# Second mixer of a two-layer block: the context's cumulative gates by a scan of products instead of a doubling ladder

## Chip, core and metric

The kernel runs on one core of one Trainium2 chip. The metric is device time of that core in microseconds (us), the median of the runs of one kernel.

The engines are named as the profile names them: PE (TensorE matmuls; PEld its weight loads), DVE (VectorE), ACT (ScalarE), POOL (GpSimd) and SP (which issues the DMAs). Each takes its instructions in the order in which the program lists them, so an instruction that waits holds back all that stand behind it on its engine.

## What is computed

The reference runs two transformer blocks of two layers each over 256 latent and 256 context tokens, 1024 wide. The change is in the second layer of the first block, whose mixer is a gated linear recurrence, forward and backward, with eight heads of 128 (cut to what matters):

```python
def _odd_mixer(h_ctx, h_lat, w_in, lower_bounds, layer, out_norm, ctx_out):
    fq, f_fwd, f_bwd, fi, fog = _split(h @ w_in, ODD_SIZES)
    q = _heads(jax.nn.silu(fq), HGRN_HEADS)
    ...
    for d, f in enumerate((f_fwd, f_bwd)):
        log_f = ...                       # log of a gate between lb and 1
        k = -jnp.expm1(log_f)
        dirs.append(_directional_scan(q, k, i, log_f, n_ctx, reverse=(d == 1)))
    ...
# recurrence in each direction:  S_t = diag(exp(g_t)) S_{t-1} + k_t v_t^T,  o_t = S_t^T q_t
# the context is scanned first from a zero state, the latent tokens go on from its final state
```

Only the latent outputs are wanted in this layer. Of the context, then, only the final state counts: the sum over its tokens of k times v, each k multiplied by all gates that come after it in the direction of the recurrence. That running product of gates over the 256 context tokens is what is computed in another way.

## The kernel before

The eight heads are worked off as four pairs. In `odd_mixer`, `proj(p)` multiplies the tokens by the weights of pair p. Its projections are fp32, made of two reduced-precision parts each: ACT casts a weight tile `raw` to `hi` (L203), DVE subtracts to get `lo` (L204), and PE runs three matmuls for each (L213 to L215; L285, L287 and L288 with the tokens as the stationary side). Out of each projection of gates ACT makes two sigmoids (L818). DVE turns them into the gates `ac` (context) and `al` (latent) on L824, and into the keys `Kc` and `Kl` on L822. Each of these tiles holds two directions, two heads and 256 tokens: 4 x 256 numbers in each of 128 partitions. `late(p)` projects the output gate and the values; PE's matmuls L337 of a stream of modulation weights (`mraw`, two buffers, 512 KB each) lie between the projections.

`hgrn_pair(p, ...)` is a ladder of eight levels. At level `lev` tokens are taken in blocks of m = 2^lev. For the latent tokens each level makes a tile of scores on PE (L909), copies it under a mask into `S` (DVE, L911), and multiplies `Kl` (L914) and `Q2` (L923) by the products of gates over a block, `tl`. For the context the same ladder runs on POOL: at each level `Kc` is multiplied by the products over blocks, `tc_` (L924), and the products are halved in number by multiplying neighbours (L929, on POOL for `tc_`, on DVE for `tl`). After eight levels each `Kc` has been multiplied by all gates behind it. POOL also adds the two directions of `Kl` (`ks`, L889). Once the ladder is through, PE multiplies `Kc` by `Q2` (L944, L945), and the read-out follows.

A scheduler sets the order of the instructions of each engine when the program is built; Python's order is only its starting point. The ladders of pairs 0 and 1 run while PE projects for the pairs behind them; the ladders of pairs 2 and 3 run interleaved with one another and with `late(2)` and `late(3)`.

Of the kernel before, what the change touches and what calls it, by code (L numbers as in the profile page):

```python
# [9 lines left out]
F32 = mybir.dt.float32  # L10
# [3 lines left out]
ALU = mybir.AluOpType  # L14
# [3 lines left out]
P = 128  # L18
# [19 lines left out]
def vw(ap, off, dims):  # L38
    return bass.AP(ap.tensor, ap.offset + off, [ap.ap[0]] + [list(d) for d in dims])
# [97 lines left out]
class Kern:  # L137
# [741 lines left out]
    def hgrn_pair(self, p, al, ac, Kl, Kc, Q2, q, V, sog, gain, mix):  # L879
        nc = self.nc  # L880
        mm = nc.tensor.matmul
        DS = 512

        def g2(name):
            return mix.tile([P, 2, 256], F32, tag=name, name=self.n(name), bufs=2)

        S = g2("S")
        ks = mix.tile([P, 2, 256], F32, tag="S256", name=self.n("ks"), bufs=2)
        nc.gpsimd.tensor_tensor(ks, Kl[:, 0], Kl[:, 1], ALU.add)  # L889
        ps = self.psum("pa")  # L890
        for h in range(2):
            for tt in range(2):
                ts = slice(tt * P, (tt + 1) * P)
                mm(ps[:, h * 256 + tt * P:h * 256 + (tt + 1) * P], ks[:, h, ts], q[:, h, ts], start=True, stop=True)
        nc.scalar.copy(S.rearrange("p h n -> p (h n)"), ps)
        for d in range(2):
            nc.vector.tensor_tensor(Q2[:, d], q, al[:, d], ALU.mult)
        tl = al.rearrange("p d h n -> p (d h n)")
        tc_ = ac.rearrange("p d h n -> p (d h n)")
        for lev in range(8):  # L900
            m = 1 << lev
            nb = DS // (2 * m)
            pat = [[2 * m, nb], [DS + m, 2], [1, m]]
            if lev < 7:
                KC = g2("KC").rearrange("p h n -> p (h n)")
                nc.scalar.copy(vw(KC, 0, [[2 * m, nb], [m, 2], [1, m]]), vw(Kl, 0, pat))
                ps = self.psum("pa")
                for b in range(4):
                    mm(ps[:, b * P:(b + 1) * P], KC[:, b * P:(b + 1) * P],  # L909
                       vw(Q2, b * P, [[2 * m, 64 // m], [DS + m, 2], [1, m]]), start=True, stop=True)  # L910
                nc.vector.copy_predicated(S.rearrange("p h (t i) -> p (h t) i", t=2),  # L911
                                          self.masks[:, lev, None, :].to_broadcast([P, 4, P]),
                                          ps.rearrange("p (t i) -> p t i", t=4))
                nc.vector.tensor_tensor(vw(Kl, 0, pat), vw(Kl, 0, pat), self.dyadic(m, DS, nb, tl, "k"), ALU.mult)  # L914
            else:
                S128 = g2("S128")
                ps = self.psum("pa")
                for h in range(2):
                    o = h * 256
                    mm(ps[:, o + P:o + 256], Kl[:, 0, h, :P], Q2[:, 1, h, P:], start=True, stop=True)  # L920
                    mm(ps[:, o:o + P], Kl[:, 1, h, P:], Q2[:, 0, h, :P], start=True, stop=True)
                nc.scalar.copy(S128.rearrange("p h n -> p (h n)"), ps)
            nc.vector.tensor_tensor(vw(Q2, 0, pat), vw(Q2, 0, pat), self.dyadic(m, DS, nb, tl, "q"), ALU.mult)  # L923
            nc.gpsimd.tensor_tensor(vw(Kc, 0, pat), vw(Kc, 0, pat), self.dyadic(m, DS, nb, tc_, "k"), ALU.mult)  # L924
            if lev < 7:
                for w, eng in (("l", nc.vector), ("c", nc.gpsimd)):
                    t2 = mix.tile([P, 2, nb], F32, tag=f"tot{w}{lev}", name=self.n("tot"), bufs=2)
                    pr = vw(tl if w == "l" else tc_, 0, [[DS // m, 2], [2, nb], [1, 2]])
                    eng.tensor_tensor(t2, pr[:, :, :, 0], pr[:, :, :, 1], ALU.mult)  # L929
                    t2 = t2.rearrange("p d n -> p (d n)")  # L930
                    if w == "l":
                        tl = t2
                    else:
                        tc_ = t2
            yield
        tag = "pl" if p > 1 else "pb"
        ss = self.psum("pb")
        oS = []
        for h in range(2):
            ps = self.psum(tag)  # L940
            for j in range(2):
                js = slice(j * P, (j + 1) * P)
                o = ps[:, j * 256:(j + 1) * 256]
                mm(o, Kc[:, 0, h, js], Q2[:, 1, h], start=True, stop=False)  # L944
                mm(o, Kc[:, 1, h, js], Q2[:, 0, h], start=False, stop=True)  # L945
            S256 = mix.tile([P, 512], F32, tag="S256", name=self.n("S256"), bufs=2)
            nc.scalar.copy(S256, ps)
            po = self.psum("pa")
            vs = slice((2 * p + h) * P, (2 * p + h + 1) * P)
            for j in range(2):  # L950
                mm(po[:, :256], V[:, j, vs], S256[:, j * 256:(j + 1) * 256], start=j == 0, stop=False,
                   skip_group_check=True)
            for tt in range(2):
                ts = slice(tt * P, (tt + 1) * P)
                mm(po[:, ts], V[:, 2 + tt, vs], S[:, h, ts], start=False, stop=False, skip_group_check=True)
                mm(po[:, ts], V[:, 3 - tt, vs], S128[:, h, ts], start=False, stop=True, skip_group_check=True)
            oS.append(self.gated_readout_rows(po[:, :256], h, gain, mix, ss))
            yield
        r = self.sm.tile([P, 8], F32, tag="rs16", name=self.n("rs"))
        self.rstd_rows(ss[:, :4], P, 4, r[:, :4])  # L960
        yield
        for h in range(2):
            bc = self.psum(tag)
            for tt in range(2):
                mm(bc[:, tt * P:(tt + 1) * P], r[:, tt * 2 + h:tt * 2 + h + 1].to_broadcast([P, P]), self.ident,
                   start=True, stop=True)
            hd = 2 * p + h
            nc.vector.tensor_tensor(oS[h], oS[h], bc[:, :256], ALU.mult)
            nc.gpsimd.tensor_tensor(sog[:, hd], oS[h], sog[:, hd], ALU.mult)
# [1172 lines left out]
```

## Time and profile before

| | |
|---|---|
| median of 3 runs | 2533.04 us (2531.86 to 2533.44) |
| the profiled execution | 2535.2 us |
| its span, from first to last instruction | 2533.4 us |
| PE busy | 2379.4 us, 94% |
| DVE busy | 1522.6 us, 60% |
| ACT busy | 967.0 us, 38% |
| POOL busy | 509.0 us, 20% |

The profiled execution is 2.2 us longer than the median and 1.8 us longer than its own span, so a difference taken from the trace can be set against the median as it stands. The ladders of the four pairs lie between about 890 and 1165 us of the span. In rows of the timeline the first two numbers are start and duration in us, "xN" is a merged run of N instructions, and square brackets give how long the engine had been idle and what ended that.

### The profile page before, as it was taken

Reading aid. Unit: us, or ns where it says so; the run is one execution under the profiler, and the core shown is the slowest. Engines: PE = TensorE matmul, PEld = TensorE weight load, DVE = VectorE, ACT = ScalarE, POOL = GpSimd, SP = SyncE. Lnnn points to the kernel's source line nnn. Section 1 sums busy time; section 2 is a strip of 40 time slices with the busy share of each in tenths; the row PEclk is TensorE's granted clock in tenths of the full one; section 3 lists DMA queues with packets and bytes.
Section 4 is the critical chain, followed back from the end, with each engine's and each line's share of the span. In section 5 each row is a group of like instructions: output and inputs, shape, how many; then the busy total and the mean of one; then the engine's idle time right before and its main releaser. Section 6 shows DMA issues by size and latency. Waiting matters only on the chain.

```text
span 2533.4 us, 40092 instructions
## 1 busy us (share of the span) xinstructions
PE 2379.4 (94%) x15813; PEld 1959.2 (77%) x15813; DVE 1522.6 (60%) x2897; ACT 967.0 (38%) x1591; POOL 509.0 (20%) x648
## 2 busy tenths in 40 slices
PE   7999988999999888889999999999999999858999
PEld 5875566888888668889799797556888889628999
DVE  5545446778853646684555642765688734586666
ACT  5523323322222423334444443443423224535543
POOL 3910012556630232230100100110000000360000
PEclk9999998999999899999999999999999999979999
DMA  8326672556553252213865432002455533976554
GB/s 295 116 90 233 219 278 61 163 164 174 155 144 95 89 190 67 75 45 141 293 187 182 170 108 67 17 18 73 140 181 179 177 100 98 210 256 224 159 184 150
DMA packets 162925, 378.05 MB, mean 149 GB/s; under 512 B 24144, under 2 KB 70096, under 8 KB 162608
## 3 DMA queue, kind: packets, MB, share of 16 engines
q1 hardware_dynamic: 159728, 368.27, 45.8%
q0 software_dynamic: 3008, 7.21, 1.0%
q8 instruction: 125, 2.05, 0.3%
q14 instruction: 64, 0.52, 0.1%
HBM read 344.75 MB, written 30.67 MB: 148 GB/s over the span
## 4 chain that ended last, share of the span: by engine, by line
PE 48%; DVE 9%; DMA 3%; ACT 2%; issue 2%; POOL 0%; DVEq 0%; ACTq 0%; POOLq 0%
PE pl L214 12%; PE pl L213 12%; PE pl L215 11%; DMA mcol<-ada_t 2%; DVE lo L204 2%; PE pm L337 1%; DVE pm L403 1%; PE pa L909 1%; PE pl L992 1%; PE pl L287 1%; PE pa L1023 1%; DMA mraw<-ada_w 1%; PE pl L285 1%; PE pl L288 1%; PE pb L1289 1%
## 5 line engine op out<-in xcount | busy, mean ns | idle before, releaser
L203 ACT CAST hi<-raw 128x1024 fp32r<-128x1024 f32 (+4 forms) x393 | 400.3, 1020 | 840.1 <-PE pl L214 510.0
L204 DVE TENSOR_TENSOR lo<-raw,hi 128x1024 fp32r<-128x1024 f32 (+4 forms) x393 | 495.7, 1263 | 348.5 <-ACT hi L203 346.3
L214 PE MATMUL pl<-X,hi 128*128 128x256 f32 (+1 forms) x2032 | 649.5, 321 | 6.5 <-POOL X L498 5.8
L213 PE MATMUL pl<-X,hi 128*128 128x256 f32 (+1 forms) x2032 | 651.9, 323 | 2.1 <-ACT X L495 1.9
L215 PE MATMUL pl<-X,lo 128*128 128x256 f32 (+1 forms) x2032 | 647.0, 319 | 0.0
L214 PEld LDWEIGHTS pl<-X,hi 128*128 128x128 f32 x2032 | 392.3, 193 | 40.1 <-POOL X L498 8.7
L213 PEld LDWEIGHTS pl<-X,hi 128*128 128x128 f32 x2032 | 391.4, 193 | 39.8 <-issue 9.0
L215 PEld LDWEIGHTS pl<-X,lo 128*128 128x128 f32 x2032 | 392.3, 193 | 32.4 <-issue 6.6
L214 PE MATMUL pl<-hl,hi 128*128 128x256 f32 (+1 forms) x1071 | 327.0, 306 | 6.6 <-DVE hl L1721 6.5
L213 PE MATMUL pl<-hh,hi 128*128 128x256 f32 (+1 forms) x1071 | 327.6, 307 | 4.7 <-ACT hh L1720 4.6
L215 PE MATMUL pl<-hh,lo 128*128 128x256 f32 (+1 forms) x1071 | 325.6, 305 | 0.0
L213 PEld LDWEIGHTS pl<-hh,hi 128*128 128x128 f32 x1071 | 202.4, 189 | 20.8 <-ACT hh L1720 5.8
L214 PEld LDWEIGHTS pl<-hl,hi 128*128 128x128 f32 x1071 | 202.7, 189 | 18.1 <-DVE hl L1721 8.4
L215 PEld LDWEIGHTS pl<-hh,lo 128*128 128x128 f32 x1071 | 202.9, 190 | 10.3 <-issue 0.8
L337 PE MATMUL pm<-mraw,s_cc 128*32 128x512 f32 x576 | 120.0, 618 | 13.2 <-DMA mraw<-ada_w 13.0
L1513 POOL TENSOR_TENSOR Ec<-PGr,bc 128x576 f32<-128x576 f32 x64 | 94.9, 1494 | 170.3 <-DMA bc<-s_w 89.1
L213 PE MATMUL pl<-M,hi 128*128 128x256 f32 (+1 forms) x416 | 122.9, 298 | 6.1 <-ACT hi L203 5.2
L215 PE MATMUL pl<-M,lo 128*128 128x256 f32 (+1 forms) x416 | 122.3, 296 | 1.2 <-DVE lo L204 1.2
L214 PE MATMUL pl<-M,hi 128*128 128x256 f32 (+1 forms) x416 | 122.6, 296 | 0.2 <-DVE M L864 0.2
L498 POOL TENSOR_TENSOR X<-nt,X 128x256 fp32r<-128x256 f32 x48 | 37.9, 790 | 415.3 <-ACT nt L497 415.3
L403 DVE SCALAR_TENSOR_TENSOR pm<-mcol,mrow 128x512 f32<-128x512 f32 x128 | 89.3, 698 | 33.3 <-DMA mcol<-ada_t 22.5
L1734 DVE TENSOR_TENSOR y<-y,pl 128x256 f32<-128x256 f32 (+1 forms) x86 | 45.1, 525 | 102.1 <-PE pl L215 101.6
(515 smaller groups left out, 3710.7 us busy)
## 6 DMA issues: line engine op xcount, KB each, us to landing
mraw<-mod_w SPq DMA_DIRECT2D x96, 512.0 KB, 5.9
raw<-f_u SPq DMA_DIRECT2D x88, 512.0 KB, 4.3
mraw<-ada_w SPq DMA_DIRECT2D x64, 512.0 KB, 6.3
raw<-p_u SPq DMA_DIRECT2D x64, 512.0 KB, 3.7
raw<-p_d SPq DMA_DIRECT2D x64, 512.0 KB, 3.6
raw<-ow_fm SPq DMA_DIRECT2D x32, 512.0 KB, 3.3
mcol<-ada_t SPq DMA_DIRECT2D x64, 256.0 KB, 3.0
raw<-f_d SPq DMA_DIRECT2D x32, 448.0 KB, 3.3
```

Of the source, the lines that this page charges most:

```text
L203: nc.scalar.copy(hi, raw)
L204: nc.vector.tensor_tensor(lo, raw, f32(hi), ALU.subtract)
L213: mm(out, w[0][:, kw, wsl], xh, start=first and a == 0, stop=False, skip_group_check=True)
L214: mm(out, w[0][:, kw, wsl], xl, start=False, stop=False, skip_group_check=True)
L215: mm(out, w[1][:, kw, wsl], xh, start=False, stop=last and a == nk - 1, skip_group_check=True)
L285: mm(o, X[0][:, kk, ts], w[0][:, k, :], start=kk == 0 and tt % per == 0, stop=False, skip_group_check=True)
L287: mm(o, X[0][:, kk, ts], w[1][:, k, :], start=False, stop=False, skip_group_check=True)
L337: nc.tensor.matmul(ps[32 * j:32 * j + 32, :], s[:, k, :], raw[:, jj * 512:(jj + 1) * 512], start=k == 0, stop=k == KT - 1, skip_group_chec ...
L403: nc.vector.scalar_tensor_tensor(self.psum("pm"), buf[:, n % 2], 1.0, s[:, v], ALU.mult, ALU.mult, accum_out=(dst if h else part)[:, v, j: ...
L498: nc.gpsimd.tensor_tensor(lo[:, k, a:b], t, f32(hi[:, k, a:b]), ALU.subtract)
L1513: nc.gpsimd.tensor_tensor(Ec[i], ff[i], cs[i], ALU.mult)
L1734: nc.vector.tensor_tensor(y[:, c, a0:b0], y[:, c, a0:b0], ps, ALU.add)
```

## The change

The context's ladder is taken out of all eight levels: POOL no longer multiplies `Kc` at each level (8 instructions for each pair) and no longer halves `tc_` (7 for each pair). In its place DVE runs four scans for each pair, one for each direction and head. A scan goes over 255 of the 256 context gates, forward for direction 0 and backward for direction 1, and replaces each by the product of itself with all before it; the second operand of the scan is a column of ones. Then POOL multiplies the keys of one direction by these products, both heads at once, shifted by one token: two instructions for each pair. In Python this stands at levels 3 and 5. The latent ladder and all matmuls are as before.

```diff
             nc.vector.tensor_tensor(vw(Q2, 0, pat), vw(Q2, 0, pat), self.dyadic(m, DS, nb, tl, "q"), ALU.mult)
-            nc.gpsimd.tensor_tensor(vw(Kc, 0, pat), vw(Kc, 0, pat), self.dyadic(m, DS, nb, tc_, "k"), ALU.mult)
             if lev < 7:
-                for w, eng in (("l", nc.vector), ("c", nc.gpsimd)):
-                    t2 = mix.tile([P, 2, nb], F32, tag=f"tot{w}{lev}", name=self.n("tot"), bufs=2)
-                    pr = vw(tl if w == "l" else tc_, 0, [[DS // m, 2], [2, nb], [1, 2]])
-                    eng.tensor_tensor(t2, pr[:, :, :, 0], pr[:, :, :, 1], ALU.mult)
...
+                t2 = mix.tile([P, 2, nb], F32, tag=f"totl{lev}", name=self.n("tot"), bufs=2)
+                pr = vw(tl, 0, [[DS // m, 2], [2, nb], [1, 2]])
+                nc.vector.tensor_tensor(t2, pr[:, :, :, 0], pr[:, :, :, 1], ALU.mult)
+                tl = t2.rearrange("p d n -> p (d n)")
+            if lev in (3, 5):
+
+                d = lev // 2 - 1
+                for h in range(2):
+                    a = vw(ac, d * DS + h * 256 + 255 * d, [[1 - 2 * d, 255]])
+                    nc.vector.tensor_tensor_scan(a, a, self.ones[:, :1].to_broadcast([P, 255]), 1.0, ALU.mult, ALU.mult)
+                ks, gs = slice(1 - d, 256 - d), slice(d, 255 + d)
+                nc.gpsimd.tensor_tensor(Kc[:, 1 - d, :, ks], Kc[:, 1 - d, :, ks], ac[:, d, :, gs], ALU.mult)
```

The lines behind it shift by one or less (L909 becomes L908, L911 becomes L910, L923 becomes L922). The order of the instructions moves in three places that matter below. In the listings a row is line, operation, output tile, input tiles and shape; the last number in a tile's name counts the tiles of the program.

POOL, the context ladder of pair 1. Before, its first part:

```order
L929 TENSOR_TENSOR tot_9122<-ac_8126 128x512
L929 TENSOR_TENSOR tot_9137<-tot_9122 128x256
L924 TENSOR_TENSOR Kc_8128<-Kc_8128,ac_8126 128x256x2
L929 TENSOR_TENSOR tot_9152<-tot_9137 128x128
L924 TENSOR_TENSOR Kc_8128<-Kc_8128,tot_9122 128x128x2x2
L929 TENSOR_TENSOR tot_9167<-tot_9152 128x64
L924 TENSOR_TENSOR Kc_8128<-Kc_8128,tot_9137 128x64x2x4
L929 TENSOR_TENSOR tot_9182<-tot_9167 128x32
L924 TENSOR_TENSOR Kc_8128<-Kc_8128,tot_9152 128x32x2x8
```

Of the 15 instructions of the pair, these 9 and 6 more, two are left, with `ks` and what follows behind them; here is all that POOL has from pair 0's second product to pair 1's `sog`:

```order
L935 TENSOR_TENSOR Kc_7587<-Kc_7587,ac_7585 128x2x255
L935 TENSOR_TENSOR Kc_8128<-Kc_8128,ac_8126 128x2x255 x2
L889 TENSOR_TENSOR ks_9083<-Kl_8127 128x512
L970 TENSOR_TENSOR sog_7583<-oS_8551,sog_7583 128x256
L970 TENSOR_TENSOR sog_7583<-oS_8571,sog_7583 128x256
```

DVE, from the last gates of pair 1 to the first score of pair 0's level 0. Before:

```order
L822 TENSOR_SCALAR Kl_8127<-sg_8355,lbt 128x256
L929 TENSOR_TENSOR tot_9120<-al_8125 128x512
L929 TENSOR_TENSOR tot_9135<-tot_9120 128x256
L204 TENSOR_TENSOR lo_8657<-raw_8654,hi_8656 128x1024
L929 TENSOR_TENSOR tot_9150<-tot_9135 128x128
L929 TENSOR_TENSOR tot_9165<-tot_9150 128x64
L929 TENSOR_TENSOR tot_9180<-tot_9165 128x32
L929 TENSOR_TENSOR tot_9195<-tot_9180 128x16
L929 TENSOR_TENSOR tot_9210<-tot_9195 128x8
L204 TENSOR_TENSOR lo_8691<-raw_8688,hi_8690 128x1024
L911 COPY_PREDICATED S_8423<-masks_7568,pa_8436 128x512
L923 TENSOR_TENSOR Q_1351_7588<-Q_1351_7588,al_7584 128x256x2
```

After the change the fourth scan (printed as SCALAR_TENSOR_TENSOR on L933) stands in that stretch; the pair's other three stand each behind an earlier group of L822 and L824, ahead of an L204:

```order
L822 TENSOR_SCALAR Kl_8127<-sg_8355,lbt 128x256
L926 TENSOR_TENSOR tot_9103<-al_8125 128x512
L933 SCALAR_TENSOR_TENSOR ac_8126<-ac_8126,ones 128x255
L204 TENSOR_TENSOR lo_8641<-raw_8638,hi_8640 128x1024
L926 TENSOR_TENSOR tot_9115<-tot_9103 128x256
L926 TENSOR_TENSOR tot_9127<-tot_9115 128x128
L926 TENSOR_TENSOR tot_9139<-tot_9127 128x64
L926 TENSOR_TENSOR tot_9154<-tot_9139 128x32
L926 TENSOR_TENSOR tot_9166<-tot_9154 128x16
L926 TENSOR_TENSOR tot_9181<-tot_9166 128x8
L204 TENSOR_TENSOR lo_8675<-raw_8672,hi_8674 128x1024
L910 COPY_PREDICATED S_8423<-masks_7568,pa_8436 128x512
```

PE, the last levels of the interleaved ladders of pairs 2 and 3. Before, the last of them stand among projections, here the end (20 projection matmuls stand ahead of the first row, and 188 behind the last score before the ladder's closing matmuls):

```order
L285 MATMUL pl_9853<-hi_9911,X_7461 128x256
L285 MATMUL pl_9854<-hi_9911,X_7461 128x256
L213 MATMUL pl_9973<-X_7461,hi_9969 128x256
L214 MATMUL pl_9973<-X_7462,hi_9969 128x256
L909 MATMUL pa_10147<-Q_1528_8804,KC_10145 128x128 x4
L909 MATMUL pa_10162<-Q_1616_9293,KC_10160 128x128
L287 MATMUL pl_9853<-lo_9912,X_7461 128x256
```

After the change the last four scores follow one another, and 236 projection matmuls stand behind them, 48 more than before:

```order
L908 MATMUL pa_9693<-Q_1602_9261,KC_9691 128x128 x4
L213 MATMUL pl_9917<-X_7461,hi_9913 128x256
L214 MATMUL pl_9917<-X_7462,hi_9913 128x256
L908 MATMUL pa_9705<-Q_1521_8788,KC_9703 128x128 x4
L908 MATMUL pa_9720<-Q_1602_9261,KC_9718 128x128 x4
L908 MATMUL pa_10091<-Q_1521_8788,KC_10089 128x128 x4
L908 MATMUL pa_10103<-Q_1602_9261,KC_10101 128x128 x4
L287 MATMUL pl_9797<-lo_9802,X_7461 128x256
```

One more thing moves, in pair 0: the loads of two modulation tiles (`mraw`) go ahead of four loads of `raw` on SP, and their matmuls L337 go with them, one group earlier on PE; the third tile of the stream still stands behind the `raw` load that waits for DVE's `lo` of `ow_v`.

## Rows read from the trace of the kernel before

**Rows 1.** The page: busy time of each engine, and the chain by engine.

```profile
PE 2379.4 (94%) x15813; PEld 1959.2 (77%) x15813; DVE 1522.6 (60%) x2897; ACT 967.0 (38%) x1591; POOL 509.0 (20%) x648
PE 48%; DVE 9%; DMA 3%; ACT 2%; issue 2%; POOL 0%; DVEq 0%; ACTq 0%; POOLq 0%
```

**Rows 2.** Windows, pair 1: stretch, length, busy of five engines, PEclk, DMA share, GB/s.

```profile
960.00:980.00 20.00, 12.49 (x92) 12.15 (x91) 17.86 (x18) 7.17 (x10) 16.18 (x15) 0.82 0.26 87
```

**Rows 3.** Timeline of PE, the long waits of pairs 0, 1, 2 and 3.

```profile
905.27 0.58 PE L287 MATMUL pl<-lo,X 128*128 128x256 f32 x1 [5.44 <-DVE lo L204]
978.35 2.05 PE L909 MATMUL pa<-Q,KC 128*128 128x128 f32 x8 [7.51 <-DVE Q L923]
1053.94 1.41 PE L909 MATMUL pa<-Q,KC 128*128 128x128 f32 x5 [7.50 <-DVE Q L923]
1111.81 3.78 PE L909 MATMUL pa<-Q,KC 128*128 128x128 f32 x16 [8.08 <-DVE S L911]
```

**Rows 4.** Timeline of DVE, pair 1, ahead of PE's wait and in it.

```profile
963.75 1.13 DVE L822 TENSOR_SCALAR Kc<-sg,lbt 128x256 f32<-128x256 f32 x1
...
965.50 2.54 DVE L929 TENSOR_TENSOR tot<-al 128x512 f32<-128x512 f32 x1
...
968.51 2.56 DVE L204 TENSOR_TENSOR lo<-raw,hi 128x1024 fp32r<-128x1024 f32 x1
970.99 3.05 DVE L929 TENSOR_TENSOR tot<-tot 128x128 f32<-128x128 f32 x5
973.98 2.13 DVE L204 TENSOR_TENSOR lo<-raw,hi 128x1024 fp32r<-128x1024 f32 x1
...
976.65 1.55 DVE L923 TENSOR_TENSOR Q<-Q,al 128x512 f32<-128x512 f32 x1
```

**Rows 5.** Timeline of POOL, the same stretch, first and last products.

```profile
965.39 2.11 POOL L924 TENSOR_TENSOR Kc<-Kc,ac 128x512 f32<-128x512 f32 x1
...
976.13 4.32 POOL L924 TENSOR_TENSOR Kc<-Kc,tot 128x512 f32<-128x512 f32 x3
```

**Rows 6.** DVE while POOL is idle: timeline, then groups (count, busy us, mean ns).

```profile
958.39 0.35 DVE L822 TENSOR_SCALAR Kc<-sg,lbt 128x256 f32<-128x256 f32 x1
...
961.96 1.22 DVE L204 TENSOR_TENSOR lo<-raw,hi 128x1024 fp32r<-128x1024 f32 x1 [2.96 <-ACT hi L203]
...
L923 DVE TENSOR_TENSOR Q<-Q,tot 128x512 f32<-128x512 f32 x7 | 4.7, 674 | 0.0
L911 DVE COPY_PREDICATED S<-masks,pa 128x512 f32<-128x512 int32 x6 | 4.4, 739 | 2.8 <-PE pa L909 2.8
...
L914 DVE TENSOR_TENSOR Kl<-Kl,al 128x512 f32<-128x512 f32 x1 | 1.1, 1104 | 0.0
...
L968 DVE TENSOR_TENSOR oS<-oS,pb 128x256 f32<-128x256 f32 x2 | 0.7, 415 | 0.0
```

**Rows 7.** POOL: the ladder's products as a group, and one `ks`.

```profile
L924 POOL TENSOR_TENSOR Kc<-Kc,tot 128x512 f32<-128x512 f32 x28 | 41.8, 1492 | 0.5
...
1078.54 1.28 POOL L889 TENSOR_TENSOR ks<-Kl 128x512 f32<-128x512 f32 x1 [22.49 <-issue]
```

**Rows 8.** Windows behind the waits of pairs 0, 1 and 3, columns as above.

```profile
905.30:911.40 6.10, 6.10 (x18) 2.63 (x18) 4.69 (x5) 0.00 (x0) 5.53 (x4) 0.50 0.52 165
...
978.40:983.10 4.70, 4.70 (x22) 4.70 (x23) 4.70 (x6) 1.54 (x2) 1.97 (x2) 0.51 0.07 26
...
1111.80:1116.20 4.40, 4.39 (x20) 4.39 (x21) 4.40 (x4) 1.25 (x2) 4.32 (x4) 0.50 0.00 0
```

**Rows 9.** DVE ahead of pair 0's wait; `mraw` from issue to landing.

```profile
903.99 1.23 DVE L204 TENSOR_TENSOR lo<-raw,hi 128x1024 fp32r<-128x1024 f32 x1
...
DMA to landing us min/median/max: 3.7/4.5/7.0
```

**Rows 10.** Windows of pairs 2 and 3 behind the wait, and their last score matmuls.

```profile
1116.20:1137.00 20.80, 20.54 (x176) 20.36 (x175) 20.55 (x33) 8.98 (x15) 0.46 (x1) 1.00 0.08 27
1137.00:1160.00 23.00, 23.00 (x194) 23.00 (x193) 9.36 (x11) 6.80 (x13) 0.00 (x0) 1.00 0.48 160
...
1136.01 1.27 PE L909 MATMUL pa<-Q,KC 128*128 128x128 f32 x10
```

More of the change, by code (lines that the diff above doesn't have):

```diff
@@ L898, in hgrn_pair @@
         tl = al.rearrange("p d h n -> p (d h n)")
-        tc_ = ac.rearrange("p d h n -> p (d h n)")
         for lev in range(8):
@@ L923, in hgrn_pair @@
             nc.vector.tensor_tensor(vw(Q2, 0, pat), vw(Q2, 0, pat), self.dyadic(m, DS, nb, tl, "q"), ALU.mult)
-            nc.gpsimd.tensor_tensor(vw(Kc, 0, pat), vw(Kc, 0, pat), self.dyadic(m, DS, nb, tc_, "k"), ALU.mult)
             if lev < 7:
-                for w, eng in (("l", nc.vector), ("c", nc.gpsimd)):
-                    t2 = mix.tile([P, 2, nb], F32, tag=f"tot{w}{lev}", name=self.n("tot"), bufs=2)
-                    pr = vw(tl if w == "l" else tc_, 0, [[DS // m, 2], [2, nb], [1, 2]])
-                    eng.tensor_tensor(t2, pr[:, :, :, 0], pr[:, :, :, 1], ALU.mult)
[L930 to L934, printed above, removed]
+                t2 = mix.tile([P, 2, nb], F32, tag=f"totl{lev}", name=self.n("tot"), bufs=2)
[9 more added lines that the diff above has]
+                nc.gpsimd.tensor_tensor(Kc[:, 1 - d, :, ks], Kc[:, 1 - d, :, ks], ac[:, d, :, gs], ALU.mult)
             yield
```

## The prediction

> **What bounds the kernel now.** I read the page first. PE is busy 94% of the span and is nearly half of the chain that ended last, POOL is 0% of it [rows 1]. Work that is taken off POOL is worth nothing by itself, then; it is worth something only where POOL's work makes PE stand still. So I went to the stretch in which the touched lines run, and there to the windows: in 20 us of pair 1 PE is busy 12.49, and DVE and POOL are both almost full [rows 2]. PE's timeline shows one long wait in each of the four pairs, 5.44, 7.51, 7.50 and 8.08 us, together 28.5 us, and each ends with an instruction of DVE [rows 3].
>
> Why is DVE late there? Its own timeline tells it [rows 4, 5, 6]. A 128x256 product with one tensor input takes 1.13 us beside POOL's ladder and 0.35 before it begins; `lo` takes 2.56 and 2.13 against 1.22; the first halving of `tl` takes 2.54, where a product of as many elements takes 0.67 with POOL idle; `Q<-Q,al` takes 1.55. On POOL the product that lies over the 2.54 us takes 2.11. Both are "busy" in those rows, but each is largely waiting for the other: from 963.75 to 978.20 us DVE needs 14.45 us for what its undisturbed rows price at about half. `S` reads PSUM beside its mask and is the exception; I give it its 0.74 throughout.
>
> **What is removed.** 15 POOL instructions in each pair, 60 in all, among them the 28 products of 1.49 us mean [rows 7]. On the path they cost nothing as POOL time; their price is what they do to DVE.
>
> **What is added.** Four scans for each pair on DVE, and two products on POOL. No row shows a scan. From below its 255 elements with two inputs are bounded by the 256-wide product with two inputs, 0.42 us, from above, far off, by the 1024-wide `lo`, 1.22 us [rows 6]. I take 0.6, nearer the row of its own width, since a running product should cost something over an independent one. Three of a pair's four scans stand ahead of a `lo` for which DVE waits idle anyway (2.96 us in pair 1) [rows 6], so that up to that length they are hidden; were that cover gone, they would cost 1.8 us a pair. The fourth stands on the path to PE's wait. The new POOL product is as wide as an old one: 1.1 to 1.5 us.
>
> [...]
>
> **Pair 1, step by step.** The gates are done at 963.75. From there to the end of `Q<-Q,al`, with undisturbed prices [rows 6]: two L822 at 0.35 make 0.70; halving to 512, at most 0.67; the fourth scan, 0.60; two `lo`, 2.44; six shorter halvings, 1.0 (none can be above the 0.42 of a 256-wide product, so 2.5 at most, and the smallest are a few elements); `S`, 0.74; `Q<-Q,al`, 1.10 (the row of `Kl<-Kl,al`, which has the same shape and step). Sum 7.25 us, end at 971.0. PE's wait began at 978.35 - 7.51 = 970.84 [rows 3]. So with POOL silent almost nothing of the wait is left. POOL is not quite silent: the product of the other direction can run earlier, while DVE waits for `hi`, but that of direction 0 becomes ready with the fourth scan and falls into this stretch, at 0 to 1.5 us. I leave 1.0 us of wait (bounds 0 and 3) and take 6.5 us.
>
> The wait also costs clock. [...] With 1 us of standstill in place of 7.5 I expect that to go. Pair 1: 6.5 + 2.3 = 8.8 us, between 4.5 (3 us left, clock still down) and 9.8. Pair 2 waits the same 7.50 us in the same order of instructions: 8.8 again.
>
> **Pair 0.** PE waits 5.44 us for a `lo` that ends at 905.22 [rows 3, 9], and then runs 6.1 us at half clock, 3 us lost [rows 8]. The `lo` comes out of a queue of DVE work slowed in the same way, and should be done just before 900. But what is late next is the modulation stream. Its third tile stands on SP behind the `raw` load that needs exactly this `lo`; so it is issued at about 899.5 and lands 3.7 to 7.0 us later, 4.5 by the median [rows 9], at about 904. PE is there at about 901.5 and waits 2 to 3 us. Two of the stream's groups are by then already done, which takes two more off what follows. Of 8.5 us I take 6, with 3 and 8 as bounds.
>
> **Pairs 2 and 3.** The wait is 8.08 us and the half clock behind it 4.4 us long [rows 3, 8]. By the same sum about 1.5 us would be left (here `ks` falls into the stretch too, 1.28 us [rows 7]), so the interleaved ladder begins 6.6 us earlier; its first levels no longer run beside POOL, which is full until 1116 [rows 8], worth 2 us, and one `lo` of 1.2 us moves out of it. But behind that DVE is the limit: 20.55 of 20.80 us busy [rows 10], while PE only fills in. The change puts 48 projection matmuls that filled in behind the ladder. At 23.00 / 194 = 0.119 us each [rows 10] they cost 5.7 us once the last scores, which end at 1137.28, are through. 6.6 + 2 + 1.2 - 5.7 = 4.1; I take 4, between 0 and 7.
>
> **Sum.** 6 + 8.8 + 8.8 + 4 = 27.6 us off the profiled execution's 2535.2 us. That lies 2.2 us over the median, and no part of the sum hangs on those 2.2, so the median goes from 2533.0 to 2505.4 us. Behind the mixer PE is the limit, and loads are issued as buffers come free, so I expect the gain to be handed on. With all lower ends the gain is 12 us, with all upper ends 34.6.
>
> **Rivals.** *The interlock stays.* Each pair keeps three POOL instructions, 1.49 + 1.49 + 1.28 = 4.3 us [rows 7]. If all of that falls on DVE's path, and a scan takes 1.22 us, the wait of pairs 1 and 2 is 0.2 + 4.3 + 0.6 = 5.1 us, the clock still falls, and each gains 2.4; pair 0 gains 3 and pair 3 nothing over its refilled order. Total 7.8: 2525 us. For it: in rows 4 and 5 every POOL product costs DVE its full length. Against it: one product of each pair is ready while DVE is idle. [...]
>
> *Nothing moves.* If PE's waits were really set by something that DVE in turn waits for, the weights or ACT's casts, they would stay: 2533 us, within 0.2%, which is about what a measurement of this kernel can tell from no change (5 us). Against it: between 963.75 and 978.20 DVE is never idle.
>
> *Slower: the scan is serial.* Each step of a scan needs the one before it, and no row has such an operation. If one took s us, each pair would pay s - 0.6 on the path and three times what exceeds the 2.96 us of cover. At s = 4 that is 3.4 + 3.1 = 6.5 us for a pair, 26 for four: from there on the change loses. At s = 5 it is 4.4 + 6.1 = 10.5, 42 us for four against a gain of 27.6: 2547 us. Against it: that would be 16 to 20 ns an element, where 0.42 us for 256 is 1.6 ns.
>
> **How the numbers follow.** Forecast 0.80, the interlock 0.11, nothing moves 0.05, serial scan 0.04. Faster by over 0.2%: 0.80 + 0.11 = 0.91; within it 0.05; slower 0.04. The range goes from the upper ends, 2533.0 - 34.6 = 2498, to the lower, 2521; what it leaves out is the rivals and a little of the forecast.
>
> **What would show it.** In the changed kernel DVE's rows of pair 1 should have the prices of rows 6, a scan 0.4 to 0.9 us, POOL some 3 to 5 us a pair, and PE's waits of pairs 1 and 2 should be under 3 us with the clock at 1.0 behind them. A wait for `mraw` should stand in pair 0, and gaps between the last scores of pairs 2 and 3. I am wrong if the scan takes several us, if DVE's 128x1024 rows still take over 2 us in those stretches, or if the gain of the waits is there but PE stands still as long elsewhere.

## The result, and the profile after

| | before | after |
|---|---|---|
| median | 2533.24 us (2531.86 to 2533.48) | 2504.7 us (2502.0 to 2515.29) |
| span of the profiled execution | 2533.4 us | 2502.5 us |
| DVE busy | 1522.6 us | 1499.1 us |
| POOL busy | 509.0 us | 453.7 us |

The ratio of after to before is 0.99, 95% interval 0.9874 to 0.9925: 19 to 32 us less. The forecast was 2505.4 us.

The long waits first. The page of the kernel after, its row of busy times, and then its waits of PE from 880 to 1150 us (what waited, for what; us in all, times, longest), against rows 3:

```profile
PE 2370.1 (95%) x15813; PEld 1951.2 (78%) x15813; DVE 1499.1 (60%) x2913; ACT 967.3 (39%) x1591; POOL 453.7 (18%) x596
```

```profile
PE pm L337 <- DMA mraw<-ada_w: 3.6, 2, 2.3
PE pa L908 <- DVE Q L922: 3.1, 3, 1.3
PE pa L908 <- DVE S L910: 2.1, 1, 2.1
```

The wait for `lo` in pair 0 is gone, and waits for the modulation stream stand in its place; the other three went from 7.51, 7.50 and 8.08 to 1.31, 1.30 and 2.10 us. In PE's timeline of after:

```profile
899.64 1.07 PE L337 MATMUL pm<-mraw,s_cc 128*32 128x512 f32 x2 [2.32 <-DMA mraw<-ada_w]
...
960.08 0.48 PE L908 MATMUL pa<-Q,KC 128*128 128x128 f32 x2 [1.31 <-DVE Q L922]
...
1027.53 0.72 PE L908 MATMUL pa<-Q,KC 128*128 128x128 f32 x4 [1.30 <-DVE Q L922]
...
1077.59 0.59 PE L908 MATMUL pa<-Q,KC 128*128 128x128 f32 x2 [2.10 <-DVE S L910]
```

DVE in pair 1, from the last gates to PE's first score, answers to rows 4. `lo` has its undisturbed price again (1.20 and 1.22 us, where rows 6 have 1.22), and only the row of six halvings is long (2.60 us, 1.64 in no_products below):

```profile
951.95 0.35 DVE L822 TENSOR_SCALAR Kl<-sg,lbt 128x256 f32<-128x256 f32 x1
952.21 0.69 DVE L926 TENSOR_TENSOR tot<-al 128x512 f32<-128x512 f32 x1
952.82 0.69 DVE L933 TENSOR_TENSOR_SCAN ac<-ac,ones 128x255 f32<-128x255 f32 x1
953.41 1.20 DVE L204 TENSOR_TENSOR lo<-raw,hi 128x1024 fp32r<-128x1024 f32 x1
954.53 2.60 DVE L926 TENSOR_TENSOR tot<-tot 128x256 f32<-128x256 f32 x6
957.07 1.22 DVE L204 TENSOR_TENSOR lo<-raw,hi 128x1024 fp32r<-128x1024 f32 x1
958.21 0.72 DVE L910 COPY_PREDICATED S<-masks,pa 128x512 f32<-128x512 int32 x1
958.83 1.10 DVE L922 TENSOR_TENSOR Q<-Q,al 128x512 f32<-128x512 f32 x1
```

Of POOL's two products in that pair the first meets an idle DVE, the second does not (against rows 5); and all 16 scans as one line (min, median and max in ns):

```profile
947.62 1.09 POOL L935 TENSOR_TENSOR Kc<-Kc,ac 128x510 f32<-128x510 f32 x1 [56.08 <-DVE ac L933]
953.58 2.50 POOL L935 TENSOR_TENSOR Kc<-Kc,ac 128x510 f32<-128x510 f32 x1 [4.87 <-DVE ac L933]
```

```profile
L933 DVE TENSOR_TENSOR_SCAN ac<-ac,ones x16: 664/684/691, 874.8 to 1070.0; 128x255 f32<-128x255 f32 x16
```

The windows behind the waits answer to rows 8 (the number third from the end is the granted clock):

```profile
899.60:902.70 3.10, 3.06 (x9) 1.40 (x10) 0.00 (x0) 0.00 (x0) 0.00 (x0) 0.51 0.76 275
960.10:964.80 4.70, 4.70 (x38) 4.58 (x39) 4.32 (x8) 2.58 (x4) 0.00 (x0) 1.00 0.18 68
1077.60:1082.00 4.40, 3.93 (x28) 3.76 (x28) 4.21 (x6) 1.29 (x2) 0.00 (x0) 1.00 0.00 0
```

To set the gain against the terms of the forecast the span is cut at marks: the starts of the 101st, 116th, 126th and 132nd of the program's 393 casts L203, which stand in the same order in before and after, and PE's first L966 (L965 before), which ends the interleaved ladders. Three of these marks in the trace of after:

```profile
873.77 1.04 ACT L203 CAST hi<-raw 128x1024 fp32r<-128x1024 f32 x1
...
954.68 1.05 ACT L203 CAST hi<-raw 128x1024 fp32r<-128x1024 f32 x1
...
1146.60 0.80 PE L966 MATMUL pl<-pack_sb,rs 128*128 128x128 f32 x5
```

In before the five marks are at 879.05, 966.74, 1042.34, 1100.76 and 1178.91 us. A piece's gain is the difference of its lengths:

| piece | forecast | measured |
|---|---|---|
| pair 0 (101st to 116th cast) | -6 | -6.78 |
| pair 1 (116th to 126th) | -8.8 | -8.15 |
| pair 2 (126th to 132nd) | -8.8 | -7.86 |
| ladders of pairs 2 and 3 (132nd cast to L966) | -4 | -4.24 |
| the mixer | -27.6 | -27.03 |

The two profiled spans differ by 30.9 us, more than that: 4.8 us of it lie ahead of the 25th cast, at 350 us, where the two programs are the same, and 2.4 us are given back right behind the mixer. In the profiled executions of this study the part ahead of the 25th cast took between 348 and 358 us, and the part behind the 201st cast, far behind the mixer, between 1147 and 1160 us. That is why the verdicts below rest on pieces between marks more than on whole times. The whole times of the kernel before lie between 2525 and 2543 us over all its executions; pieces in which two kernels list the same work agree to 0.1 us (the first three pieces of refill, below, against those of after). Each piece is nevertheless read from one profiled execution of a kernel.

### The profile page after: what moved, and what is told of

The parts are those of the page before. It is cut to its first block, busy times and chain, and to the rows that moved or that the text cites. A ratio compares the mean times of both kernels' runs of the same rounds, so it can differ in the third digit from the quotient of the medians.

```text
span 2502.5 us, 40056 instructions
## 1 busy us (share of the span) xinstructions
PE 2370.1 (95%) x15813; PEld 1951.2 (78%) x15813; DVE 1499.1 (60%) x2913; ACT 967.3 (39%) x1591; POOL 453.7 (18%) x596
## 4 chain that ended last, share of the span: by engine, by line
PE 80%; DVE 10%; DMA 4%; ACT 3%; issue 2%; POOL 1%; SPq 0%; DVEq 0%; ACTq 0%; POOLq 0%
PE pl L213 19%; PE pl L214 18%; PE pl L215 18%; PE pm L337 3%; PE pl L993 2%; DVE lo L204 2%; DMA mcol<-ada_t 2%; PE pl L287 1%; PE pl L288 1%; PE pl L285 1%; DVE pm L403 1%; PE pa L669 1%; PE pb L1024 1%; PE pl L1015 1%; PE pa L85 1%
## 5 line engine op out<-in xcount | busy, mean ns | idle before, releaser
L203 ACT CAST hi<-raw 128x1024 fp32r<-128x1024 f32 (+4 forms) x393 | 400.6, 1020 | 841.5 <-PE pl L214 496.7
L204 DVE TENSOR_TENSOR lo<-raw,hi 128x1024 fp32r<-128x1024 f32 (+4 forms) x393 | 489.0, 1246 | 343.8 <-ACT hi L203 341.8
L337 PE MATMUL pm<-mraw,s_cc 128*32 128x512 f32 x576 | 119.2, 622 | 13.4 <-DMA mraw<-ada_w 13.1
```

Source lines behind the costliest of these rows:

```text
L203: nc.scalar.copy(hi, raw)
L204: nc.vector.tensor_tensor(lo, raw, f32(hi), ALU.subtract)
L337: nc.tensor.matmul(ps[32 * j:32 * j + 32, :], s[:, k, :], raw[:, jj * 512:(jj + 1) * 512], start=k == 0, stop=k == KT - 1, skip_group_chec ...
```

## Experiments

**The order of after, the ladder back on POOL.** While DVE still runs the scans, POOL again works a ladder of 15 instructions for each pair, on a tile that nobody reads.

```diff
+        tc_ = tl
+        Kz = mix.tile([P, 2, 2, 256], F32, tag="Kz", ...)
+        nc.gpsimd.memset(Kz, 1.0)
...
+            nc.gpsimd.tensor_tensor(vw(Kz, 0, pat), vw(Kz, 0, pat), self.dyadic(m, DS, nb, tc_, "k"), ALU.mult)
+            if lev < 7:
+                nc.gpsimd.tensor_tensor(t3, pc[:, :, :, 0], pc[:, :, :, 1], ALU.mult)
+                tc_ = t3.rearrange("p d n -> p (d n)")
```

> The changed kernel, with the 15 ladder instructions of each pair put back on POOL beside it, on a tile of their own that nobody reads (first operand al in place of ac). DVE, PE, ACT and SP keep the changed kernel's order word for word. Theory (DVE and POOL wait for each other): DVE's rows slow down again (lo over 2 us, the first halving of al over 1.5 us in the four stretches), PE's waits of pairs 1 and 2 come back to 6 to 9 us each with half clock behind them, and the time goes back to 2525 to 2540 us. Rival (the order of PE, SP and DVE that moved with the change made the gain, or the shorter chain of POOL): nobody waits for these instructions and the order is the changed one, so 2503 to 2508 us, waits of pairs 1 and 2 near the changed kernel's 1.3 us.

Measured: 2537.64 us, ratio to before 1.0023 (1.0004 to 1.0041); mixer 8.2 us longer than before. PE's waits came back a little longer than the 6 to 9 us expected. The waits of PE, and DVE in pair 1:

```profile
PE pa L911 <- DVE Q L925: 18.6, 2, 9.3
PE pa L911 <- DVE S L913: 8.7, 1, 8.7
PE pl L287 <- DVE lo L204: 5.8, 1, 5.8
```

```profile
960.80 1.52 DVE L935 TENSOR_TENSOR tot<-al 128x512 f32<-128x512 f32 x1
962.25 2.01 DVE L942 TENSOR_TENSOR_SCAN ac<-ac,ones 128x255 f32<-128x255 f32 x1
964.18 1.56 DVE L204 TENSOR_TENSOR lo<-raw,hi 128x1024 fp32r<-128x1024 f32 x1
965.67 4.71 DVE L935 TENSOR_TENSOR tot<-tot 128x256 f32<-128x256 f32 x6
970.33 2.10 DVE L204 TENSOR_TENSOR lo<-raw,hi 128x1024 fp32r<-128x1024 f32 x1
```

Nobody waits for what this ladder computes, and yet the whole gain is gone: a scan takes 2.01 in place of 0.69, the six halvings 4.71 in place of 2.60.

**The order of before, no ladder.** The counterpart: the kernel before without its POOL ladder, and nothing in its place, so that the context's keys are not decayed.

```diff
-            nc.gpsimd.tensor_tensor(vw(Kc, 0, pat), vw(Kc, 0, pat), self.dyadic(m, DS, nb, tc_, "k"), ALU.mult)
             if lev < 7:
-                for w, eng in (("l", nc.vector), ("c", nc.gpsimd)):
+                for w, eng in (("l", nc.vector),):
```

> The kernel before without POOL's ladder: the decay of the context keys is left out, and neither scans nor new products stand in its place. DVE, PE, ACT and SP keep the order of before word for word. Theory (POOL's ladder slows DVE): PE's waits of pairs 1, 2 and 3 go from 7.5, 7.5 and 8.1 to under 1.5 us, pair 0's long wait goes or becomes one for a DMA of 1 to 4 us, no half clock in pairs 1 and 2, gain between the marks of the mixer 30 to 38 us, time 2495 to 2503 us; pairs 2 and 3, which keep their 48 filling projections, gain 7 to 11 us where the changed kernel gained 4.2. Rival (the moved order made the gain): with the order of before the waits stay at 7.5 us and the time at 2528 to 2534 us.

Measured: 2494.02 us, ratio 0.9852 (0.983 to 0.9875); pieces -7.89, -9.22, -8.92 and -8.87, mixer -34.9 us; the time is 1 us under the range expected, the pieces are inside theirs. No wait of PE for DVE is longer than 0.8 us:

```profile
PE pm L337 <- DMA mraw<-ada_w: 2.6, 4, 1.0
PE pa L909 <- DVE S L911: 0.8, 1, 0.8
PE pa L909 <- DVE Q L923: 0.7, 3, 0.2
```

The two runs together separate order and ladder. With the ladder on POOL neither order gains (the order of before is 0 by definition, that of after +8.2 us), without it both do (-34.9 and -27.0). The order of after carries scans and products as well, so the differences between the two orders are not the price of the order alone. But the moved order explains no gain at all; taking the ladder off POOL explains all of it.

**Only writes on POOL.** As the first experiment, but with memsets in place of the ladder, save for its first product.

```diff
+            if lev == 0:
+                nc.gpsimd.tensor_tensor(vw(Kz, 0, [[1, 512]]), tl[:, :512], tl[:, 512:], ALU.mult)
+            else:
+                nc.gpsimd.memset(vw(Kz, 0, [[1, 512]]), 1.0)
+                nc.gpsimd.memset(vw(Kz, 0, [[1, 512]]), 1.0)
+            if lev < 7:
+                nc.gpsimd.memset(vw(Kz, 0, [[1, 2 * nb]]), 1.0)
```

> As idle_ladder, but all of POOL's extra work in a pair save its first product are memsets (two of 512 elements for each product, 0.52 us each in the trace of before, and one for each halving): POOL is about as long busy in the same stretches, and writes, but reads nothing. Every other engine keeps the changed kernel's order. Theory (it is POOL's reading of SBUF beside DVE's two-input instructions that makes them wait for each other): DVE's rows keep their undisturbed prices but for some 1 us a pair by the first product; PE's waits of pairs 1 and 2 are 1.3 to 2.6 us; time 2504 to 2512 us. Rival (any instruction of POOL stands in DVE's way, writes too): as idle_ladder, waits of 6 to 9 us in pairs 1 and 2, 2530 to 2540 us.

Measured: 2514.39 us, ratio 0.9923 (0.9901 to 0.9945); mixer -22.0, that is 5.0 us over after: 0.1 in pair 0, 1.2 in each of pairs 1 and 2, and 2.5 in the last piece, where PE waits 3.23 us in place of 2.10 and runs on at a granted clock of 0.50. The range for the time was missed by 2 us. DVE and POOL in pair 1:

```profile
951.88 1.41 DVE L822 TENSOR_SCALAR Kl<-sg,lbt 128x256 f32<-128x256 f32 x1
...
955.53 2.71 DVE L934 TENSOR_TENSOR tot<-tot 128x256 f32<-128x256 f32 x6
958.19 1.23 DVE L204 TENSOR_TENSOR lo<-raw,hi 128x1024 fp32r<-128x1024 f32 x1
```

```profile
957.63 0.53 POOL L927 MEMSET Kz<- 128x512 f32 x1
958.21 0.53 POOL L928 MEMSET Kz<- 128x512 f32 x1
```

Beside memsets `lo` takes 1.23 and a memset 0.53 (0.52 elsewhere): neither waits. The one extra product of POOL, which reads, costs DVE 1.06 us on `Kl` (1.41 against 0.35); it took 1.29 itself. So in this run neither POOL's being busy nor its writing stands in the way. What a product does and a memset does not is to read tiles from SBUF. The run shows the difference between the two instructions; that the reading makes it is inferred.

**After without the two products.**

```diff
-                nc.gpsimd.tensor_tensor(Kc[:, 1 - d, :, ks], Kc[:, 1 - d, :, ks], ac[:, d, :, gs], ALU.mult)
```

> The changed kernel without the two POOL products of each pair (the context keys keep their undecayed values; the scans stay). Every other engine keeps its order. Theory (a POOL product that falls into DVE's stretch costs DVE its own length): in pairs 1 and 2 the six halvings behind the first lo take 1.5 us in place of 2.60, PE's waits go from 1.31 and 1.30 to about 0.2 us, pair 3's 2.10 to about 1, pair 0's wait for mraw stays near 2 us; sum 3 to 5 us, time 2499 to 2503 us. Rival (the products are hidden, and the remaining waits are DVE's own work): waits stay at 1.3 us, time 2504 to 2506 us.

Measured: 2503.26 us, ratio 0.9884 (0.9861 to 0.9907); mixer -31.8, which is 4.8 us less than after: 1.90, 0.90, 0.90 and 1.06 us in the four pieces. In pair 1 the halvings are short:

```profile
952.66 1.64 DVE L926 TENSOR_TENSOR tot<-tot 128x256 f32<-128x256 f32 x6
```

2.60 against 1.64: the one product that falls there costs DVE 0.96 us, nearly its length of 1.09. The whole time alone, 1.4 us under that of after with overlapping intervals, would not have shown it.

**Every scan twice.**

```diff
                     nc.vector.tensor_tensor_scan(a, a, self.ones[:, :1].to_broadcast([P, 255]), 1.0, ALU.mult, ALU.mult)
+                    nc.vector.tensor_tensor_scan(z, a, self.ones[:, :1].to_broadcast([P, 255]), 1.0, ALU.mult, ALU.mult)
```

> The changed kernel with every scan followed by a second one of the same length into a scratch tile: 16 more on DVE at 0.68 us each. In pair 1 one of the four extra scans stands where DVE waits idle, three behind the gates, in the stretch that PE waits for; pair 2 has two to three there. Theory (a scan costs its 0.6 us of DVE time where DVE is late, and nothing where DVE is idle): PE's wait of pair 1 grows by 1.8 us to about 3.1, pair 2's by 1.2 to 1.8, pair 0 still waits for mraw, pair 3 grows by 1.5 to 3; with a fall of the clock 1 to 2 us more at each; time 2507 to 2518 us. Rival (scans are not on the path at all): 2503 to 2506 us. Rival (every scan costs its length, 16 x 0.68 = 11 us, and more by the clock): over 2516 us.

Measured: 2506.38 us, ratio 0.989 (0.9868 to 0.9912); mixer -22.6, 4.5 us over after. The time lies between the range expected and that of the first rival, and decides nothing; the pieces do. PE's wait in pair 1 is 2.08 us in place of 1.31, so three more scans on that path cost 0.77, not the 1.8 expected: of the six small halvings only three are left in that stretch. In the last piece the price is 3.5 us. Scans are on the path where DVE is late, but 16 of them, 10.9 us of DVE time, cost 4.5.

**Pairs 2 and 3 refilled.** The ladder's steps are spread over the late projections.

```diff
-        for _ in range(12):
+        for _ in range(8):
             next(two)
+        self.bg["l"] = two
         late(2)
         late(3)
+        del self.bg["l"]
-        for _ in range(10):
+        for _ in range(6):
             next(two)
...
-        ... tick='m')
+        ... tick='ml')
```

> The changed kernel with the code of pairs 2 and 3 written in another order: 8 steps of their ladders ahead of the late projections and one more behind each of these projections' eight tiles, in place of 12 ahead and 10 behind. PE then has blocks of 24 and 48 projection matmuls between the last scores, which stood back to back. Theory (the forecast's term for the moved projections: they no longer fill PE while DVE works on the last levels): PE's gaps of 0.43, 0.76 and 0.66 us between the last scores go; pairs 2 and 3 gain 1.5 to 3.5 us more than the changed kernel, time 2501 to 2504 us. Rival (DVE is the bound there, and what PE does meanwhile doesn't matter): within 1 us, 2504 to 2506 us.

Measured: 2503.21 us, ratio 0.9885 (0.9861 to 0.9909); the last piece gains 6.31 where after gained 4.24, so 2.1 us more; of the three gaps between the last scores those of 0.76 and 0.66 us are gone, and one of 0.41 is left. The whole time cannot tell the two kernels apart.

**Scans and products late.** Four kernels tried to earn what the two products and the fourth scan still cost. In the first all of them stand at level 6, where the scores of level 5 release them; in the second those of the ladders of pairs 0 and 1 stand at level 7; the other two add the refilled order. The edit of the first (the second has `lev == (7 if p < 2 else 6)`):

```diff
-            if lev in (3, 5):
-                d = lev // 2 - 1
+            if lev == 6:
+                one = self.sm.tile([P, 1], F32, tag="one", ...)
+                nc.vector.tensor_scalar(one, S[:, 0, :1], 0.0, 1.0, ALU.mult, ALU.add)
+                for d in range(2): ...
-                    nc.vector.tensor_tensor_scan(a, a, self.ones[:, :1].to_broadcast([P, 255]), 1.0, ALU.mult, ALU.mult)
+                        nc.vector.tensor_tensor_scan(a, a, one.to_broadcast([P, 255]), 1.0, ALU.mult, ALU.mult)
```

> The changed kernel with all four scans and both products of a pair moved to level 6 of its ladder: the scans' second operand is a column of ones that DVE makes from the scores of level 5, so that none can run earlier. The stretch ahead of PE's first score then holds neither scan nor product, and PE's order in pairs 2 and 3 is that of before, with the 48 projections among the last scores. Theory (what the change leaves is the price of products and of the fourth scan in that stretch and of the moved projections, 7.7 us by the runs no_ladder and no_products): PE's waits of pairs 1, 2 and 3 are those of no_ladder, under 1 us, and 33 to 35 us are gained between the mixer's marks; time 2492 to 2499 us. Rival (scans and products are on the path wherever they stand): PE waits 2 to 4 us a pair for the closing matmuls' keys, 2501 to 2510 us.

> late_scans and refill together. Theory: without scans among the gates the order of pairs 2 and 3 already fills PE, whose gaps there are 1.7 us in no_ladder (0.83, 0.23 and 0.64 us), so that at most these go: 0 to 1.7 us faster than late_scans. Rival (the ladder's steps, tied to the late projections' tiles, now wait for those): 1 to 5 us slower than late_scans.

> late_scans with the scans of the ladders of pairs 0 and 1 one level later, behind the scores and products of level 6, so that the closing scores of level 7 no longer wait for them; pairs 2 and 3 as in late_scans. Theory (in late_scans PE's two waits of 2.38 us for the scores of level 7 are four scans that stand ahead of level 6 on DVE): both waits go or fall under 0.5 us, 4 to 5 us are gained against late_scans between the mixer's marks, 31 to 32 us against before; time 2497 to 2504 us. Rival (the closing matmuls wait instead, for the keys from scans and products): waits of 2 to 5 us behind level 7, time as late_scans, 2503 to 2510 us.

> late_level7 and the refilled order of pairs 2 and 3 together. Theory: the gains add, since they lie in different stretches: 4 to 5 us of the two waits of level 7 and about 1.5 us of the wait for lo in pairs 2 and 3 against late_scans; between the mixer's marks 32 to 34 us less than before; time 2494 to 2502 us, the best of all that leave nothing out. Rival: a gain in one place is lost to a wait in the next, 2502 to 2508 us.

| kernel | median | ratio to before | mixer |
|---|---|---|---|
| after | 2504.7 | 0.99 (0.9874 to 0.9925) | -27.0 |
| late_scans | 2508.86 | 0.9905 (0.9884 to 0.9927) | -27.0 |
| late_refill | 2505.25 | 0.9887 (0.9866 to 0.9909) | -29.8 |
| late_level7 | 2506.93 | 0.9894 (0.9874 to 0.9914) | -26.2 |
| late_level7_refill | 2504.75 | 0.9889 (0.9867 to 0.9912) | -27.1 |

My theory fell in late_scans, in late_level7 and in late_level7_refill, which was to gain 32 to 34 us and be the best: each time the waits ahead of the first scores did go, and others came. In late_scans PE waits for `Q` ahead of the scores of level 7, in the other two for the closing matmuls' keys, as the rival had it. late_refill gained 2.7 us on late_scans, more than the 0 to 1.7 expected. The last row, of late_level7's DVE, shows that there too scans and a POOL product stand in each other's way:

```profile
976.71 0.46 PE L928 MATMUL pa<-Q,Kl 128*128 128x128 f32 x2 [2.38 <-DVE Q L931]
```

```profile
978.86 0.70 PE L946 MATMUL pb<-Q,Kc 128*128 128x256 f32 x2 [2.79 <-POOL Kc L911]
```

```profile
973.81 3.46 DVE L909 TENSOR_TENSOR_SCAN ac<-ac,one 128x255 f32<-128x255 f32 x4
```

Four scans one behind the other would take 2.5 us undisturbed (an estimate: 4 x 0.60, the step from one row to the next, and 0.08), here they take 3.46. The place that the change gives them, among the gates, where DVE waits for `hi`, is as cheap as any that I tried, within half a us: late_scans equals after, and late_refill is 0.5 us better than refill.

**The modulation stream out of pair 0.** The stream's steps start with pair 1, first in after alone, then with late_level7_refill; `late` gets the stream's name as an argument, and pair 0 none.

```diff
-        late(0)
+        late(0, '')
```

> The changed kernel with the modulation stream's steps taken out of pair 0's late projections: its loads and matmuls come with the later pairs. Theory (what is late in pair 0 is the third tile of that stream, which waits on SP behind a raw load): PE's waits of 2.32 and 1.26 us for mraw in pair 0 go, with the 3.4 us of half clock behind the first, 3 to 5 us gained up to the mark of pair 1, of which the later pairs give back what the moved matmuls cost where nothing else waits, nothing in the sum, since they were PE work before too; time 2499 to 2503 us. Rival (behind mraw PE would have waited for lo as before): the wait stays 1 to 3 us under another name, 2503 to 2507 us.

> late_level7_refill with the modulation stream taken out of pair 0's late projections as in no_mods0. Theory: pair 0's waits for mraw, 0.74 and 1.09 us in late_scans, go too; 1 to 2 us less than late_level7_refill, 2492 to 2501 us. Rival (the stream's steps that come later stand where pairs 2 and 3 need SP and PE): 0 to 3 us more than late_level7_refill.

Measured: no_mods0 2507.4 us, ratio 0.9898 (0.9869 to 0.9927), mixer -29.8; all_three 2502.03 us, ratio 0.9873 (0.985 to 0.9896), mixer -34.3. (Work moves across the inner marks here, so only the mixer as a whole can be compared.) Without the stream PE has no long wait in pair 0; the stream's waits come later, 0.91 and 1.45 us in place of 2.32 and 1.26. The times missed what was expected: that of no_mods0 by 4 us (its executions run from 2500.5 to 2516.7, and 2.8 us gained in the mixer stand against 3 to 5 expected), that of all_three by 1. The mixer of all_three is 7.3 us shorter than that of after, but its median is only 2.7 us lower and the intervals overlap: whether it beats after is not settled. Most of the rest of the 7.3 us is lost behind the 201st cast, which takes 1156.2 us here and 1149.6 in after; both lie within the spread given above, so it stays open whether that is more than scatter.

## Why the prediction was right, step by step

**DVE and POOL slow each other, and that is what the change removes.** Right, by the two runs that hold the order and change the ladder: a scan takes 2.01 us in idle_ladder and 0.69 in after, and in after a POOL product takes 2.50 us beside the halvings and 1.09 where DVE is idle. A POOL product costs DVE about its own length (0.96 and 1.06 us, for products of 1.09 and 1.29), memsets cost it nothing (`lo` 1.23 us beside them and 1.22 without); by what mechanism, no run shows. The rival that the interlock stays, that is, that each POOL instruction left still costs DVE its length, was right in kind and wrong in size: what is left costs 4.8 us of the mixer, where the rival had 20.

**A scan.** 0.6 assumed, 0.684 measured (median of 16 in after, 0.664 to 0.691). The 256-wide product with two inputs took 0.42 [rows 6]; a scan of 255 takes as long as the 512-wide product ahead of it in pair 1, 0.69 us. The serial scan of several us is excluded.

**Pair 1, the sum of 7.25 us.** From the start of the first L822 (951.69) to the end of `Q<-Q,al` (959.93) it took 8.24. Of the miss of 1.0 us, 0.6 is the term for six halvings (1.0 assumed, 1.64 by no_products), and 0.96 is the product of direction 0, which I had put into the wait and not into the sum (1.0 us of wait assumed, 1.31 and 1.30 measured); neighbouring rows overlap by some hundredths each, which gives the rest back. The clock stayed up, as assumed: in the 4.70 us behind the wait it is 1.00 and PE runs 38 matmuls, where before had 0.51 and 22 [rows 8]. No run shows the forecast's 2.3 us of clock as such; 4.70 x 0.49 = 2.3 us is an estimate from that window of before. 8.8 us were forecast for each of pairs 1 and 2, 8.15 and 7.86 measured: right in the mechanism, up to 0.9 us too high in size.

**Pair 0.** The new wait was forecast by name and size: 2 to 3 us for the third tile of the modulation stream; measured 2.32, then 3.1 us at half clock. 6 us forecast, 6.78 measured, in part by luck: the terms named there (8.5 of old wait and clock, less 2 to 3 of new wait, plus 2) come to about 8, I took 6 without saying what the other 2 are, and the half clock behind the new wait, some 1.5 us by the window's 3.1 us at 0.51, is named nowhere. no_mods0 confirms that nothing else was late there.

**Pairs 2 and 3.** 4 us forecast, 4.24 measured. The steps can be read off PE's rows. In before the last score ahead of the projections stands at 1136.01 [rows 10], and the projections end at the first of these rows:

```profile
1159.67 0.83 PE L909 MATMUL pa<-Q,KC 128*128 128x128 f32 x6
1162.04 0.46 PE L920 MATMUL pa<-Q,Kl 128*128 128x128 f32 x2 [0.64 <-DVE Q L923]
```

In after the first row is that last score, and the projections end at the second:

```profile
1099.15 1.16 PE L908 MATMUL pa<-Q,KC 128*128 128x128 f32 x8 [0.66 <-ACT KC L905]
1128.69 0.38 PE L919 MATMUL pa<-Q,Kl 128*128 128x128 f32 x2
```

Up to the first score behind the wait 6.1 us are gained (6.6 assumed), from there to the end of the last score ahead of the projections 2.8 (2 + 1.2 assumed), and the projections take 6.0 more (5.7 assumed), 28.4 us in place of 22.4. Behind them another 1.3 us are gained, which the forecast had not: in before six scores and a wait of 0.64 still stood there. So each step was right in kind and within half a us in size, and that the sum came closer still is luck. refill, whose PE has some of the moved projections back among the scores, gains 2.1 us on after, as it should. POOL is not out of the way in this stretch: a product and `ks` still fall on DVE, and one `lo` takes 2.29 us. A 128x1024 row of over 2 us was one of the prediction's signs of being wrong; it came true for this one row, beside the instructions that POOL has left.

**The gain is handed on.** Nearly. Behind the mixer 2.42 us are given back, which the forecast had not. PE waits there for `mraw` in both kernels, for 1.09 and 0.76 us before and 1.06 and 1.34 after, and of the two only in after does the clock fall behind it. A window of after, and then the same work before:

```profile
1192.80:1199.60 6.80, 6.26 (x19) 1.59 (x13) 4.42 (x18) 1.71 (x4) 0.86 (x1) 0.50 0.62 248
```

```profile
1225.40:1232.00 6.60, 4.92 (x30) 2.68 (x28) 4.44 (x15) 3.71 (x8) 0.87 (x1) 1.00 0.60 242
```

What is given back goes with the clock and not with the length of the mixer. From the mixer's end to the 150th cast the six profiled executions in which the clock stays at 1.00 (before, no_ladder, no_products, late_scans, late_level7, late_level7_refill) take 59.4 to 60.4 us, and the eight in which it falls to half on the way 61.1 to 62.9, after among them with 62.9. idle_ladder gained nothing in the mixer and takes 62.4, no_ladder gained the most and takes 59.7. Why the clock falls there in some kernels and not in others is open.

**Range and chances.** 2504.7 lies near the forecast of 2505.4, closer than the terms deserve, and that is luck: the mixer was missed by 0.6 us, its pieces by up to 0.9, and the executions of after alone scatter over 13 us.

## What to carry to other kernels

Where DVE and POOL are both "busy", compare the same instruction with and without the other engine beside it; work that nobody waits for cost the whole gain here (idle_ladder, mixer +8.2 us against before where after has -27.0), and one POOL product cost DVE about its own length (0.96 us for 1.09, 1.06 for 1.29). Such work is best removed (no_ladder, -34.9 us), made a write (memset_ladder, -22.0), or put where the other engine idles (POOL's first product in pair 1 of after, 1.09 us, against 2.50 for the second). This was seen with POOL products that read SBUF and with DVE's two-input instructions (`lo` 2.10 us in idle_ladder and 1.22 in after) and L822 (1.41 us in memset_ladder and 0.35 in after); DVE's masked copy of scores from PSUM kept its price (0.71 us in before, 0.72 in after). To see who is late when such work goes, name for each wait the instruction that would come last next, loads included, and price the filler that the scheduler moves. Differences of a few us are read between marks in the trace, not from whole times.

## What the runs showed that the prediction did not have

- POOL's memsets run beside DVE's instructions with neither waiting (0.53 against 0.52 us, `lo` 1.23 against 1.22), while one POOL product that reads holds up even a DVE instruction with a single tensor input (L822, 1.41 in place of 0.35 us; 1.13 beside the whole ladder in rows 4).
- The clock does not fall behind every wait of a given length. In memset_ladder PE waits 3.03 us for `mraw` in pair 0 and 2.50 us in pair 1 and runs on at 1.00 both times, and waits 3.23 us ahead of the ladders of pairs 2 and 3 and runs on at 0.50; in after it waits 2.32 us in pair 0 and runs on at 0.51. The windows of memset_ladder behind its waits in pair 1 and ahead of pairs 2 and 3:

```profile
961.20:965.90 4.70, 4.70 (x38) 4.57 (x39) 4.31 (x8) 2.57 (x4) 3.83 (x10) 1.00 0.18 71
1081.10:1085.50 4.40, 4.40 (x21) 4.40 (x22) 3.71 (x6) 1.31 (x2) 3.84 (x10) 0.50 0.00 0
```

- Taking the scans out of the stretch ahead of the first scores gained nothing: what they cost in pairs 1 and 2 (0.90 us each by the products, and 0.2 by the scans, no_products against no_ladder) came back as one wait of 2.4 to 2.8 us at the ladder's end.
